# A scheduler's price for a one-pass matmul: 2,400 columns a microsecond, or what the trace shows

## The chip, the cores and the metric

The kernel runs on one core of a Trainium2 chip. The metric is device microseconds (us) of one execution. The trace is one profiled execution on the same core; its times are us from the first instruction. TensorE (PE) multiplies, VectorE (DVE) and ScalarE (ACT) do elementwise work, GpSimd (POOL) does small tensors and issues some DMAs, SyncE (SP) issues the weights' DMAs.

## The reference

Three transformer layers over 256 tokens of width 1024, all in fp32, one after the other:

```
block 1: h = rms_norm(x); u,q,k,v = split(h @ w_in)
         y = [pool_mixer(u), causal attention(q,k,v, 8 heads, T5 bias)] @ w_out
         x = x + rms_norm(y); x = x + rms_norm(conv_ffn(rms_norm(x)))
         x = x + (p @ w_ple) * sigmoid(x @ w_ple_gate)
block 2: u = x @ w_in; y = [short conv, sliding-window attention with sinks] @ w_out
         x = layer_norm(a*x + y); x = layer_norm(a*x + swiglu(x))
block 3: u = x @ w_in; y = [gated linear attention, latent attention with rope] @ w_out
         x = layer_norm(a*x + y); x = layer_norm(a*x + swiglu(x))
```

Nearly all work is fp32 matrix products of 256 tokens with weight matrices, which are read once from HBM (158 MB).

## The kernel before

Each fp32 product is made of three one-pass products in the short format fp32r (`mm3`): both operands are split into a rounded part hi and a rest lo, and hi*hi, hi*lo and lo*hi are added in PSUM. Weights come in units of 512 KB (`get`, l.488): SP's DMA fills one of four buffers `raw`; a cast makes hi (`hl<-raw`, by ACT or, as an alternative, by DVE, where its name is CAST), and a DVE subtraction makes lo (`hl<-raw,hl`). Ten split units (`hl`) form a ring. A chunk of activations against weights (`achunk`) is 24 matmuls of 128x256 (`ps<-hT,hl`); row products and the FFNs also use 128x512 (`ps<-hl,hT`, `ps<-hl,yh`).

In the attention of blocks 1 and 2 a pair of heads follows the chunk pair that makes its q and k. A head (`head`, l.741) is: q·k on PE (`ps<-wk,wk` in block 1, `ps<-g,g` in block 2), a row maximum on DVE (`ISA`), exponential and scaling on ACT and DVE (`g`), three transposes on PE (`ps<-c_ident,g`), evacuation (`pt`), and the product with v (`ps<-pt,vp`). Between q·k and the transposes PE works on chunks of the next weights: I call those matmuls filler. k of a pair is evacuated from PSUM by DVE (`wk<-ps,g`, wk_80; q is wk_82).

All calls are recorded first (`Recorder`). `cost` (l.133) gives each instruction an estimated duration. `add` (l.163) joins matmuls that follow each other on one PSUM tile into a group until the group's estimate reaches `BLOCK` = 0.7 us. `issue` (l.245) is a list scheduler: it sums PE's estimates to due times for all other work, then picks again and again the instruction that can start first by its own clock, on PE within 16 us of the next one in program order; a hi cast goes to DVE where its estimated end there is over 0.2 us earlier (`worth`, l.310). Every engine's instructions are then emitted from l.412 in the order of those estimated starts, so nearly all rows of the trace carry L412. The estimate decides the order only; the waits of the chip are real.

Of the kernel before, what the change touches and what calls it, by code (L numbers as in the profile page):

```python
# [96 lines left out]
class Recorder:  # L97
# [35 lines left out]
    def cost(self, eng, method, out, k, ins):  # L133

        n = out.free_size()
        if method == "dma_start":
            b = out.size() * 4 if callable(out.size) else out.size * 4
            return (1.05 if eng == "POOL" else 0.1), None, b / 360e3
        if eng == "PE":
            if method == "transpose":  # L140
                return n * 2 / 2400.0, None, 0
            m = ins[0].free_size()
            if ins[-1].dtype != F32:
                return max(n, 2 * m) / 2400.0, None, 0
            return (max(4 * n, 4 * m) if n > 32 else 90) / 2400.0, None, 0
        psum = any(x.space == PSUM for x in ins)
        if eng == "ACT":
            d = ((61 if psum else 112) + n) / 1200.0
            for p in ("bias", "scale", "accum_out"):
                if isinstance(k.get(p), bass.AP) and p != "scale":  # L150
                    d += 0.09
            f = k.get("func")
            return d, TABLE.get(f), 0
        if eng == "DVE":
            sc = 0.0625 * sum(isinstance(k.get(p), bass.AP) for p in ("scalar", "scalar1", "scalar2")) * (method != "tensor_tensor_reduce")
            if method in ("tensor_scalar", "tensor_copy", "memset") and not psum and out.space != PSUM:
                return sc + (66 + n / 2) / 960.0, None, 0
            return sc + (66 + n) / 960.0, None, 0
        if method == "memset":
            return 0.04 + n / 1900.0, None, 0  # L160
        return 0.14 + n * 2.15e-3 + (0.4 if k.get("op") == ALU.pow else 0), None, 0
# [1337 lines left out]
```

## Time and profile before

| what | us |
|---|---|
| runs | 878.39, 880.99, 881.13 (median 880.99) |
| the profiled execution | 879.77 |
| its span, first to last instruction | 878.0 |
| PE busy | 861.4 (98%) |
| DVE busy | 672.1 (77%) |
| ACT busy | 505.8 (58%) |
| POOL busy | 62.8 (7%) |

The mean granted TensorE clock is 0.995 of full. Blocks lie at about 0 to 290 us (attention to 100), 290 to 600 (attention 337 to 380) and 600 to the end (its mixers 608 to 656). Matmuls overlap in the trace, so the time of one is read from the start of one row to the start of the next, not from its duration.

### The profile page before, as it was taken

The page shows a single profiled execution, that of the slowest core. Times are in us where ns is not written, and L with a number is a line of the kernel's source. Part 1 is how long each engine was busy: PE and PEld are TensorE (multiplying, and loading weights), DVE is VectorE, ACT ScalarE, POOL GpSimd, SP SyncE. Part 2 cuts the span into 40 slices and gives each one's busy share as a digit, 9 for nine tenths or more (in the row PEclk, how much of TensorE's full clock was granted, in tenths as well). Part 3 has the DMA queues.
Part 4 walks back from the last instruction along what each step waited for, and adds up shares of the span by engine and source line. Part 5 has one row for each costly group of instructions (what it writes and reads, how often), then busy time and mean ns, then how long its engine had stood idle before and what let it go on. Part 6 is the DMA issues. An engine that isn't in the chain of part 4 may idle for free.

```text
span 878.0 us, 14363 instructions
## 1 busy us (share of the span) xinstructions
PE 861.4 (98%) x5182; PEld 740.2 (84%) x5182; DVE 672.1 (77%) x1421; ACT 505.8 (58%) x1086; POOL 62.8 (7%) x99
## 2 busy tenths in 40 slices
PE   8999999999999999999999999999999999999996
PEld 6898788888888889988888888888878888888885
DVE  5898889988884888868877776668996887666644
ACT  5488666665554567745655555446764666555521
POOL 2500100000000000001000000012421100000000
PEclk9999999999999999999999999999999999999998
DMA  8668574776663676527766656536542686666501
GB/s 297 200 190 263 171 245 143 221 224 188 191 213 97 179 222 206 177 66 237 257 201 190 192 185 189 176 107 210 166 137 76 233 270 191 190 189 185 185 19 48
DMA packets 45767, 160.81 MB, mean 183 GB/s; under 512 B 5544, under 2 KB 6360, under 8 KB 45696
## 3 DMA queue, kind: packets, MB, share of 16 engines
q1 hardware_dynamic: 42624, 151.21, 55.0%
q0 software_dynamic: 2640, 8.10, 2.9%
q8 instruction: 40, 0.66, 0.3%
q10 hardware_dynamic: 432, 0.58, 0.2%
q14 instruction: 31, 0.25, 0.1%
HBM read 158.43 MB, written 1.44 MB: 182 GB/s over the span
## 4 chain that ended last, share of the span: by engine, by line
PE 90%; DVE 3%; DMA 3%; issue 2%; ACT 1%; SPq 1%; POOL 0%; POOLq 0%; DVEq 0%
PE ps L412 90%; DMA raw<-in_w_dram 2%; DVE g L412 1%; DVE hl L412 1%; SPq L412 1%; DMA wk<-in_pT_dram 1%; ACT g L412 1%; DVE wk L412 1%; POOL sm L412 0%; DVE x L412 0%; POOLq L1495 0%; ACT L412 0%; ACT wk L412 0%; ACT hl L412 0%; DVE sm L412 0%
## 5 line engine op out<-in xcount | busy, mean ns | idle before, releaser
L412 DVE TENSOR_TENSOR hl<-raw,hl 128x512 fp32r<-128x512 f32 (+1 forms) x570 | 377.3, 689 | 45.0 <-ACT hl L412 39.3
L412 PE MATMUL ps<-hT,hl 128*128 128x512 f32 (+1 forms) x2400 | 401.5, 325 | 2.1 <-ACT hl L412 1.5
L412 PEld LDWEIGHTS ps<-hT,hl 128*128 128x128 f32 x2400 | 350.6, 190 | 44.9 <-issue 2.3
L412 ACT ACTIVATE hl<-raw 128x512 fp32r<-128x512 f32 (+1 forms) x518 | 309.4, 623 | 104.5 <-PE ps L412 65.4
L412 PE MATMUL ps<-hl,yh 128*128 128x512 f32 (+2 forms) x1146 | 259.4, 379 | 1.7 <-DVE yh L412 1.7
L412 PEld LDWEIGHTS ps<-hl,yh 128*128 128x128 f32 x1146 | 202.7, 188 | 40.9 <-DVE yh L412 2.3
L412 PE MATMUL ps<-hl,hT 128*128 128x512 f32 (+2 forms) x720 | 166.0, 385 | 1.1 <-ACT hl L412 1.0
L412 PEld LDWEIGHTS ps<-hl,hT 128*128 128x128 f32 x720 | 129.8, 188 | 27.2 <-ACT hl L412 2.4
L412 ACT ACTIVATE g<-ps 128x256 f32<-128x256 f32 (+6 forms) x156 | 59.4, 388 | 97.0 <-PE ps L412 96.7
L412 DVE TENSOR_TENSOR g<-ps,g 128x256 f32<-128x256 f32 x112 | 47.5, 424 | 49.9 <-ACT g L412 49.7
L412 POOL TENSOR_TENSOR sm<-sm,c_mhalf 128x1 f32<-128x1 f32 (+2 forms) x19 | 18.2, 957 | 515.9 <-DVE sm L412 515.9
L412 ACT ACTIVATE g<-g 128x256 f32<-128x256 f32 (+1 forms) x76 | 31.7, 423 | 16.4 <-DVE g L412 13.0
L412 ACT ACTIVATE yh<-g 128x256 fp32r<-128x256 f32 x57 | 23.6, 416 | 29.2 <-DVE g L412 29.2
L412 DVE CAST hl<-raw 128x512 fp32r<-128x512 f32 (+1 forms) x52 | 23.2, 449 | 17.4 <-PE ps L412 14.7
L412 ACT ACTIVATE wk<-wk,sm 128x1024 f32<-128x1024 f32 (+1 forms) x8 | 9.0, 1127 | 47.3 <-DVE sm L412 47.3
L412 DVE SCALAR_TENSOR_TENSOR wk<-x,ps 128x1024 f32<-128x1024 f32 (+2 forms) x9 | 9.7, 1073 | 32.2 <-PE ps L412 32.2
L412 ACT ACTIVATE g<-g,sm 128x256 f32<-128x256 f32 (+1 forms) x66 | 28.9, 456 | 7.2 <-DVE sm L412 6.9
L412 DVE TENSOR_TENSOR yh<-g,yh 128x256 fp32r<-128x256 f32 x66 | 27.7, 422 | 0.6 <-ACT yh L412 0.5
L412 DVE SCALAR_TENSOR_TENSOR g<-g,c_fm,g 128x255 f32<-128x255 f32 (+2 forms) x52 | 24.7, 480 | 0.9
L412 ACT ACTIVATE hT<-ps 128x512 fp32r<-128x512 f32 x25 | 14.2, 597 | 16.8 <-PE ps L412 16.7
L412 ACT ACTIVATE wk<-ps 128x1024 f32<-128x1024 f32 (+4 forms) x14 | 9.8, 704 | 23.5 <-PE ps L412 21.7
L412 PE MATMUL ps<-c_ident,g 128*128 128x128 f32 (+2 forms) x118 | 19.3, 276 | 1.5 <-DVE g L412 1.4
(121 smaller groups left out, 438.5 us busy)
## 6 DMA issues: line engine op xcount, KB each, us to landing
raw<-in_w_dram SPq DMA_DIRECT2D x277, 512.0 KB, 4.1
row<-in_rows_dram POOLq DMA_DIRECT2D x11, 512.0 KB, 5.3
raw<-in_w_dram SPq DMA_DIRECT2D x4, 432.0 KB, 3.2
x<-in_x_dram SPq DMA_DIRECT2D x2, 512.0 KB, 8.3
row<-vd POOLq DMA_DIRECT2D x8, 128.0 KB, 5.5
raw<-in_w_dram SPq DMA_DIRECT2D x3, 256.0 KB, 3.3
raw<-in_w_dram SPq DMA_DIRECT2D x2, 384.0 KB, 3.3
wk<-in_xT_dram SPq DMA_DIRECT2D x1, 512.0 KB, 7.3
```

The lines of the kernel that those rows point to most:

```text
L412: o.names.append(getattr(e, method)(*map(placed, a), **{p: placed(x) for p, x in k.items()}))
```

## The change

One line of `cost`: the estimate of a one-pass product (moving operand of n columns, stationary operand of m).

```
             m = ins[0].free_size()
             if ins[-1].dtype != F32:
-                return max(n, 2 * m) / 2400.0, None, 0
+                return max(n, 2 * m + 14) * 0.4427e-3, None, 0
             return (max(4 * n, 4 * m) if n > 32 else 90) / 2400.0, None, 0
```

For 128x256 with m = 128 the estimate goes from 0.1067 to 0.1195 us, for 128x512 from 0.2133 to 0.2267 us. A group of `BLOCK` = 0.7 us of 128x256 matmuls closes at 6 (0.717) instead of 7 (0.747), so a chunk of 24 is four groups of 6 instead of 7, 7, 7, 3. Transposes and the two-engine estimates keep their numbers. The instructions are the same but for the hi casts: 77 of them are on DVE now, 52 before. PE's order differs in the attention of blocks 1 and 2, around transposes of rows and at the start of block 3; in the FFNs PE's order is the same and other engines' orders differ.

First place: block 1, PE, the first pair of heads. hl_67 and hl_68 are chunks of the next weights, wk_80 and wk_82 the heads' k and q, g_94 the first head's probabilities.

```order
-L412 MATMUL ps<-hT_77,hl_67 128x256 x14
+L412 MATMUL ps<-hT_77,hl_67 128x256 x12
 L412 MATMUL ps<-wk_80,wk_82 128x128
 L412 MATMUL ps<-wk_80,wk_82 128x256
 L412 MATMUL ps<-wk_80,wk_82 128x128
 L412 MATMUL ps<-wk_80,wk_82 128x256
-L412 MATMUL ps<-hT_77,hl_67 128x256 x10
-L412 MATMUL ps<-hT_77,hl_68 128x256 x21
+L412 MATMUL ps<-hT_77,hl_67 128x256 x12
+L412 MATMUL ps<-hT_77,hl_68 128x256 x18
 L412 MATMUL ps<-c_ident,g_94 128x128 x3
```

q·k stands two matmuls earlier, and 30 matmuls instead of 31 stand between it and the first transposes.

On DVE the same place, before: the evacuation of k (wk_80), then up to the first row maximum (ISA).

```order
L412 TENSOR_TENSOR hl_68<-raw_66,hl_68 128x512
L412 TENSOR_TENSOR wk_80<-ps,g_102 128x256
L412 TENSOR_TENSOR yh_86<-g_107,yh_86 128x256
L412 TENSOR_TENSOR hl_70<-raw_64,hl_70 128x512
L412 SCALAR_TENSOR_TENSOR g_107<-g_106,g_103 128x256
L412 TENSOR_TENSOR hl_69<-raw_63,hl_69 128x256
L412 ISA g_94,sm_116<-ps,row_83 128x128
```

And now:

```order
L412 TENSOR_TENSOR hl_68<-raw_66,hl_68 128x512
L412 TENSOR_TENSOR yh_86<-g_107,yh_86 128x256
L412 TENSOR_TENSOR hl_70<-raw_64,hl_70 128x512
L412 SCALAR_TENSOR_TENSOR g_107<-g_106,g_103 128x256
L412 TENSOR_TENSOR hl_69<-raw_63,hl_69 128x256
L412 SCALAR_TENSOR_TENSOR g_106<-g_105,g_104 128x256
L412 TENSOR_TENSOR wk_80<-ps,g_102 128x256
L412 TENSOR_TENSOR hl_71<-raw_65,hl_71 128x512
L412 TENSOR_TENSOR hl_69<-raw_63,hl_69 128x256
L412 TENSOR_TENSOR yh_87<-g_107,yh_87 128x256
L412 TENSOR_TENSOR hl_70<-raw_64,hl_70 128x512
L412 ISA g_94,sm_116<-ps,row_83 128x256
```

The evacuation of k stands behind five instructions that it stood ahead of, and four more stand between it and the row maximum.

Second place: POOL at the end of block 1's attention. sm_150 to sm_161 are the small power operations of the norms' scales, wk_81 the load of p.

```order
 L412 TENSOR_TENSOR sm_154<-sm_153,c_mhalf 128x1
+L412 DMA wk_81<-in_pT_dram 128x512
 L412 TENSOR_TENSOR sm_157<-sm_156,c_mhalf 128x1
-L412 DMA wk_81<-in_pT_dram 128x512
 L412 TENSOR_TENSOR sm_161<-sm_160,c_mhalf 128x1
```

The load of p is issued ahead of the power operation that it stood behind.

Third place: block 2, PE, the second pair of heads. g_104 and g_102 are the probabilities of its two heads, pt and vp the product with v.

```order
-L412 MATMUL ps<-hT_77,hl_70 128x256 x7
+L412 MATMUL ps<-hT_77,hl_70 128x256 x6
 L412 MATMUL ps<-c_ident,g_104 128x128 x3
-L412 MATMUL ps<-hT_77,hl_70 128x256 x14
+L412 MATMUL ps<-hT_77,hl_70 128x256 x12
 L412 MATMUL ps<-c_ident,g_102 128x128 x3
-L412 MATMUL ps<-hT_77,hl_70 128x256 x3
 L412 MATMUL ps<-pt_179,vp_178 128x256 x3
 L412 MATMUL ps<-pt_179,vp_178 128x128 x3
```

The transposes stand one matmul earlier for the first head and three for the second.

## Rows read from the trace of the kernel before

**Rows 1.** The page: busy time by engine; two of the costliest groups (casts).
```profile
PE 861.4 (98%) x5182; PEld 740.2 (84%) x5182; DVE 672.1 (77%) x1421; ACT 505.8 (58%) x1086; POOL 62.8 (7%) x99
...
L412 ACT ACTIVATE hl<-raw 128x512 fp32r<-128x512 f32 (+1 forms) x518 | 309.4, 623 | 104.5 <-PE ps L412 65.4
...
L412 DVE CAST hl<-raw 128x512 fp32r<-128x512 f32 (+1 forms) x52 | 23.2, 449 | 17.4 <-PE ps L412 14.7
```

**Rows 2.** Waits of PE: what for; us in total, times, longest.
```profile
PE ps L412 <- DVE g L412: 2.8, 3, 1.5
PE ps L412 <- ACT hl L412: 2.4, 3, 1.5
```

**Rows 3.** Windows: us, busy time (instructions) of each engine, clock, DMA share, GB/s.
```profile
340.00:380.00 40.00, 39.99 (x328) 37.55 (x326) 35.55 (x111) 28.89 (x82) 1.79 (x5) 1.00 0.46 148
...
620.00:660.00 40.00, 38.41 (x611) 31.22 (x610) 38.03 (x107) 27.99 (x79) 14.01 (x17) 1.00 0.47 148
700.00:740.00 40.00, 40.00 (x220) 34.42 (x219) 32.65 (x64) 25.70 (x56) 0.00 (x0) 1.00 0.72 236
```

**Rows 4.** Timeline of PE, block 1: start, us, engine, line, operation, count.
```profile
43.30 0.93 PE L412 MATMUL ps<-wk,wk 64*128 64x128 f32 x8
44.16 3.98 PE L412 MATMUL ps<-hT,hl 128*128 128x256 f32 x31
47.97 0.82 PE L412 MATMUL ps<-c_ident,g 128*128 128x128 f32 x6
...
62.03 3.98 PE L412 MATMUL ps<-hT,hl 128*128 128x256 f32 x31
65.85 0.49 PE L412 MATMUL ps<-c_ident,g 128*128 128x128 f32 x3
```

**Rows 5.** Timeline of DVE, block 1, up to the first head's row maximum.
```profile
30.98 0.85 DVE L412 CAST hl<-raw 128x512 fp32r<-128x512 f32 x1
...
38.85 0.42 DVE L412 SCALAR_TENSOR_TENSOR wk<-ps,g 128x256 f32<-128x256 f32 x1 [0.28 <-PE ps L412]
...
41.91 0.41 DVE L412 TENSOR_TENSOR wk<-ps,g 128x256 f32<-128x256 f32 x1
42.24 0.69 DVE L412 TENSOR_TENSOR yh<-g,yh 128x256 fp32r<-128x256 f32 x1
...
44.25 0.29 DVE L412 CUSTOM_DVE_ANT_0 g<-ps,row 128x128 f32<-128x128 f32 x1
```

**Rows 6.** Timeline of ACT, block 1: the scaling of the probabilities before the transposes.
```profile
47.01 1.19 ACT L412 ACTIVATE g<-g,sm 128x256 f32<-128x256 f32 x3
...
65.07 1.19 ACT L412 ACTIVATE g<-g,sm 128x256 f32<-128x256 f32 x3
```

**Rows 7.** Timeline of ACT, block 2: the same scaling.
```profile
343.27 0.79 ACT L412 ACTIVATE g<-g,sm 128x256 f32<-128x256 f32 x2
...
354.93 0.50 ACT L412 ACTIVATE g<-g,sm 128x256 f32<-128x256 f32 x1
```

**Rows 8.** Timeline of PE, block 2: transposes of a pair's other head.
```profile
344.46 0.52 PE L412 MATMUL ps<-c_ident,g 128*128 128x128 f32 x3
...
355.43 0.49 PE L412 MATMUL ps<-c_ident,g 128*128 128x128 f32 x3
```

**Rows 9.** Timeline of POOL ahead of the load of p.
```profile
96.36 0.93 POOL L412 TENSOR_TENSOR sm<-sm,c_mhalf 128x1 f32<-128x1 f32 x1 [6.17 <-DVE sm L412]
```

**Rows 10.** The chain that ended last, in order of time: start, us, what.
```profile
97.25 5.79 DMA wk<-in_pT_dram
```

**Rows 11.** Timeline of PE: where it waits, with the wait in brackets.
```profile
103.42 2.58 PE L412 MATMUL ps<-hl,yh 128*128 128x512 f32 x10 [1.73 <-DVE yh L412]
105.83 1.04 PE L412 MATMUL ps<-c_ident,wk 128*128 128x128 f32 x8
...
625.88 0.61 PE L412 MATMUL ps<-c_ident,g 128*96 128x128 f32 x4 [0.94 <-DVE g L412]
...
629.68 1.05 PE L412 MATMUL ps<-c_ident,g 128*96 128x128 f32 x8 [0.43 <-DVE g L412]
```

More of the change, by code (lines that the diff above doesn't have):

```diff
@@ L143, in cost @@
             if ins[-1].dtype != F32:
-                return max(n, 2 * m) / 2400.0, None, 0
+                return max(n, 2 * m + 14) * 0.4427e-3, None, 0
             return (max(4 * n, 4 * m) if n > 32 else 90) / 2400.0, None, 0
```

## The prediction

> **What bounds the kernel now.** I read the page's busy times first: PE is busy 861.4 us of the span of 878.0, every other engine has room over the whole [rows 1]. Then the waits of PE: 2.8 us for DVE's `g`, 2.4 for ACT's `hl` [rows 2], and one wait of 1.73 us for p at 103.42 [rows 11]; 6.9 us in these together. That is the most that a better order can win, since the matmuls stay the same. Then the windows: in an FFN (700 to 740) PE is busy 40.00 of 40 us and DVE 32.65; in the attention of block 2 39.99 and 35.55; at the start of block 3 PE falls to 38.41 and DVE is at 38.03, so there DVE bounds [rows 3]. Last the timelines of PE, DVE and ACT around each attention head, to see by how much PE's operands are ready before PE takes them. The reader is to see that PE's queue hardly ever waits, and that in the attention it does so by a hair: operands come just in time.
>
> **The change part by part.** Nothing is computed that was not; only order changes, and 25 more hi casts go to DVE. So each term is a wait of PE that appears, or one that goes.
>
> *The estimate itself.* 31 matmuls of 128x256 take from 44.16 to 47.97, 0.123 us each with the handover to the transposes [rows 4]. The old estimate was 0.1067, the new one is 0.1195: the plan's PE now runs nearly as the chip's. The Trainium skill (TensorE: Matmul & The Clock Gate, "Wait — 56ns, not 53.3ns?") gives a start-to-start of columns by 2.4 GHz plus about 2.5 ns for a warm array, 0.109 us for 256 columns as an estimate; by it the old number would be right and the new one 10% too long. The row disagrees, and the measurement decides. By the page's number the plan would now give PE too little filler, and by the row it gives what the plan thinks right; either way less than before.
>
> That is what I expect to cost time. The scheduler fills PE between q·k and the transposes with as many matmuls as it believes the softmax to take. With 0.1067 it put 31 there, which lasted 3.81 us on the chip; with 0.1195 it puts 30 or fewer. The softmax has not become faster, so the old error of PE's price covered an error of the softmax's.
>
> *Block 1, first pair.* q·k starts at 43.30 [rows 4]; k's evacuation, its last operand, ran from 41.91 for 0.41 us [rows 5], ready at 42.32, a margin of 0.98. After: PE comes two matmuls earlier (2 x 0.123), at 43.06. On DVE the evacuation stands behind five more instructions. Four of them took 42.24 to 44.25, 2.01 us, the fifth I count at 0.33, the spacing of 41.91 to 42.24 for its shape: 2.34. Against it, the cast that took 0.85 is replaced by one of the usual 0.45, and DVE's gap of 0.28 can be filled [rows 1, 5]. The evacuation is ready at about 42.32 + 2.34 - 0.40 - 0.28 = 43.98, and PE waits 0.9 (0 if the five do not hold it up, 1.6 if nothing is saved).
> Four more instructions then stand before the row maximum, two subtractions of weights, half a subtraction and one of `yh`, near 1.95 us by the same rows, so it starts at about 45.9 rather than 44.25. The transposes need the first scaling on ACT, which ended about 47.45 (47.01 and a third of 1.19) [rows 6], 3.2 after the row maximum; so 49.1 after. PE, late by the first wait, comes to them after q·k and 30 matmuls: 43.98 + 0.86 + 30 x 0.123 = 48.5. It waits 0.6. First pair: 1.5.
>
> *Block 1, later pairs.* At 65.85 the transposes follow 31 matmuls that began at 62.03 [rows 4]; their operand ended near 65.5 on ACT (65.07 and a third of 1.19) [rows 6], a margin of 0.3. Now 24 matmuls stand there: 7 x 0.123 = 0.86 earlier, a wait of 0.55. Two places have this pattern (here and at the last pair, where 18 matmuls of 512 columns become 12 and one product with v): 1.1. Block 1 together +2.6; bounds 0 (DVE and ACT come earlier by as much) and +4.
>
> *Block 2.* The second head's transposes at 355.43 [rows 8] start in the moment in which ACT ends their operand, 354.93 + 0.50 [rows 7]. In the new order they stand three matmuls earlier, 0.37 of wait; two pairs are like this, 0.7. In the first pair the transposes at 344.46 [rows 8] stand nine matmuls and the product with v earlier, over 1.1 us; their operand ended at 344.06 (343.27 + 0.79) [rows 7], a margin of 0.40: 0.7. Together +1.4; bounds 0 and +2.5.
>
> *The load of p.* POOL issues it at 97.25, behind a power operation that began at 96.36 [rows 9]; it takes 5.79 us [rows 10], and PE waits 1.73 for it [rows 11]. Issued ahead of the power it lands 0.89 earlier. PE's new order also puts four matmuls of 512 columns before the product with p, at (105.83 - 103.42) / 10 = 0.24 each, 0.96 [rows 11]. Both together remove the wait. But the transposes at 105.83 need that power and a chain behind the landing; if they stay there, only the 0.96 is won, if they come 0.89 earlier all of 1.73. The power now stands behind the issue, so I take 0.2 of it: -1.15; bounds -1.73 and 0.
>
> *Start of block 3.* DVE is busy 38.03 of 40 us [rows 3]; between 608 and 652 it gets two or three more casts, at 0.449 [rows 1] +0.9 to +1.35, and subtractions of weights move ahead of the rope's copies that the transposes at 625.88 and 629.68 wait for. I take +1.2. Lower bound: those two waits go, -(0.94 + 0.43) = -1.37 [rows 11]. Upper: a cast beside POOL took 0.85 [rows 5], and POOL is busy 14.01 us of that window [rows 3]; 3 x 0.85 = +2.55. The Trainium skill (GPSIMD Engine Reference, the table of its properties) says that GpSimd's interfaces to SBUF are shared with VectorE; the cast's 0.85 against 0.449 agrees, and by that rule +2.55 would be the likelier end.
>
> *What I cost at nothing.* The other casts that move: in the FFNs DVE has 7 us of room in 40 and PE none [rows 3], and 10 casts there are 4.5 us. If that cover were gone, PE would wait for `hl`. Moved transposes of x rows: DVE's order moves with them; bounds 0 and +1.5.
>
> Sum: +2.6 + 1.4 - 1.15 + 1.2 = +4.05. On the profiled execution's 879.77 us that makes 883.8. That execution lies 1.2 below the median of the runs shown, 880.99, and between their ends.
>
> **The rivals.**
> Faster: the right price lets the plan release producers in time. Its place is where PE is waited for now: the wait for p goes wholly (1.73), and the two at block 3 with it (1.37): 879.77 - 3.1 = 876.7. For it speaks that the load is in fact issued earlier; against it that DVE in block 3 gets more work, not less. It decides if the attention's operands come earlier by more than PE does (0.4 to 0.9 us a pair), so that no new wait opens.
> No change: PE's 861.4 us stay, new waits of a few tenths are filled where the ends of products overlap, and the gain at p (1.15) pays for the rest: 879 to 881. For it speaks that PE waits under 7 us now, although hundreds of instructions stand in an order that was planned with a wrong price; against it the margins of 0 to 0.4 us.
> Much slower: DVE becomes the bound through the attention of block 1 and block 3 as well, since casts and subtractions stand before the row maxima: the upper ends, 4 + 2.5 + 0 + 2.55 = 9, 888.8. Against it: DVE still has 4.5 us of room in 40 in block 2's attention [rows 3], and a queue that is late there catches up.
>
> **How the numbers follow.** About 0.3% (2.6 us) is what a measurement of this kernel can tell from no change. Forecast, a loss of 2.6 to 6 us: 0.40. No change: 0.35, since half of the terms rest on margins that I read to 0.1 us and DVE's queue may catch up. Faster: 0.17, its working gives -3.1, beyond that bound. Much slower: 0.08. So faster 0.17, same 0.35, slower 0.48. The range reaches to 877.5, into the faster rival, and to 888.5, near the sum of the upper ends; the forecast's own range is 882.4 to 886.
>
> **What would show it right or wrong.** Right: PE's waits for DVE and ACT in 40 to 80 and 340 to 370 rise to some 4 us, the first at q·k near 43; the wait before the product with p is gone, and the transposes after it wait a little; DVE in 620 to 660 is at 39 or more. Wrong: the transposes of the attention still start without a wait, because the scaling on ACT ends earlier than it does now, or the time falls under 877.5, which would need waits gone that I hold to be DVE's own work.

## The result and the profile after

| | before | after |
|---|---|---|
| median of the runs on one chip (us) | 880.65 (4 runs, 878.39 to 881.13) | 892.08 (4 runs, 890.02 to 894.56) |
| ratio | | 1.0137, 95% interval 1.0114 to 1.0160 |
| span of the profiled execution | 878.0 | 892.7 |
| mean granted clock in it | 0.995 | 0.990 |
| waits of PE, sum of the view | 7.7 | 15.4 |

The kernel became 11.4 us slower: the direction forecast, near three times the 4.05 forecast, and outside the range of 877.5 to 888.5. The profiled execution of after is the slowest of its four, 894.56, and lies 14.7 above that of before in its span.

From the page of after, busy time by engine and the group of casts on DVE, against [rows 1]:

```profile
PE 868.9 (97%) x5182; PEld 744.9 (83%) x5182; DVE 679.6 (76%) x1439; ACT 497.2 (56%) x1068; POOL 62.3 (7%) x99
...
L412 DVE CAST hl<-raw 128x512 fp32r<-128x512 f32 (+1 forms) x77 | 33.1, 434 | 23.2 <-PE ps L412 20.8
```

The same 5182 matmuls keep PE busy 7.5 us longer: some of them ran at a lower clock. By the mean granted clocks, 0.990 of 892.7 us and 0.995 of 878.0, an estimate of 4.5 us at most goes there. The rest is waiting. Most of the loss is not the clock: the run of after at 890.02 us had a mean granted clock of 0.996 and was still 9.4 slower than the median of before. The longest of PE's waits in after, against [rows 2] (what for; total, times, longest):

```profile
PE ps L412 <- ACT g L412: 4.5, 5, 3.4
PE ps L412 <- DVE wk L412: 4.3, 2, 3.9
...
```

Two waits stand out, 3.9 for `wk` and 3.4 for ACT's `g`. The first is at q·k of block 1's first pair. Timeline of PE in after, against [rows 4]:

```profile
45.84 1.66 PE L412 MATMUL ps<-wk,wk 64*128 64x128 f32 x8 [3.93 <-DVE wk L412]
47.42 5.68 PE L412 MATMUL ps<-hT,hl 128*128 128x256 f32 x30
52.94 0.49 PE L412 MATMUL ps<-c_ident,g 128*128 128x128 f32 x3
```

Two things are to be seen: the wait, and that q·k and 30 matmuls then take 7.10 us up to the transposes. Before they took 47.97 - 43.30 less one matmul of 0.123, 4.55 [rows 4]; so 2.55 us go in the clock. Windows of after show it (us, busy time of PE, PEld, DVE, ACT, POOL, then the granted clock), and with them those of [rows 3]:

```profile
45.00:51.00 6.00, 5.16 (x24) 4.51 (x25) 5.21 (x21) 3.47 (x12) 1.04 (x2) 0.50 0.96 266
340.00:380.00 40.00, 39.32 (x328) 37.16 (x327) 34.86 (x103) 26.56 (x72) 1.94 (x5) 1.00 0.51 157
620.00:640.00 20.00, 16.46 (x118) 15.27 (x118) 19.13 (x44) 16.81 (x35) 7.72 (x10) 0.97 0.69 217
640.00:660.00 20.00, 19.92 (x472) 15.62 (x473) 17.63 (x39) 6.05 (x14) 7.14 (x11) 0.86 0.39 120
```

After PE's idle stretch the granted clock is 0.50, the level of 1.2 GHz, for the six microseconds shown; after the idle stretch in 620 to 640 it falls to a mean of 0.86 in the next 20. What PE waited for is on DVE. Its timeline in after, against [rows 5]:

```profile
29.95 0.43 DVE L412 CAST hl<-raw 128x512 fp32r<-128x512 f32 x1 [1.13 <-DMA raw<-in_w_dram]
...
43.43 0.41 DVE L412 TENSOR_TENSOR yh<-g,yh 128x256 fp32r<-128x256 f32 x1
43.76 0.68 DVE L412 TENSOR_TENSOR hl<-raw,hl 128x512 fp32r<-128x512 f32 x1
44.36 0.41 DVE L412 SCALAR_TENSOR_TENSOR g<-g,g 128x256 f32<-128x256 f32 x1
44.70 0.41 DVE L412 TENSOR_TENSOR hl<-raw,hl 128x256 fp32r<-128x256 f32 x1
45.03 0.41 DVE L412 SCALAR_TENSOR_TENSOR g<-g,g 128x256 f32<-128x256 f32 x1
45.37 0.41 DVE L412 TENSOR_TENSOR wk<-ps,g 128x256 f32<-128x256 f32 x1
...
47.58 0.41 DVE L412 CUSTOM_DVE_ANT_0 g<-ps,row 128x256 f32<-128x256 f32 x1
...
48.47 0.16 DVE L412 TENSOR_SCALAR sm<-sm 128x2 f32<-128x2 f32 x1
```

k's evacuation starts at 45.37, before at 41.91: 3.46 later. The five instructions ahead of it take 1.94 (43.43 to 45.37). Most of the rest comes from the start of the stretch, where DVE now waits 1.13 for the transfer of a weight that it is to cast; what follows that cast was 1.75 late. On ACT the exponentials stand behind two casts that wait for a transfer as well:

```profile
47.98 1.15 ACT L412 ACTIVATE hl<-raw 128x512 fp32r<-128x512 f32 x2 [2.08 <-DMA raw<-in_w_dram]
49.04 0.49 ACT L412 ACTIVATE g<-g,sm 128x256 f32<-128x256 f32 x1
...
49.53 0.39 ACT L412 ACTIVATE g<-g,sm 128x128 f32<-128x128 f32 x1
```

These casts cost little here: the operand that the first exponential needs from DVE (`sm`, at 48.47) is ready at 48.63, and it starts at 49.04. The delay is DVE's, whose first row maximum starts at 47.58, before at 44.25 [rows 5].

Block 3 has a wait of the same kind. PE in after, against [rows 11]:

```profile
632.65 4.03 PE L412 MATMUL ps<-hl,yh 128*128 128x384 f32 x21
640.08 1.91 PE L412 MATMUL ps<-c_ident,g 128*96 128x128 f32 x8 [3.40 <-ACT g L412]
```

DVE in after, then in before:

```profile
634.28 1.89 DVE L412 TENSOR_TENSOR hl<-raw,hl 128x512 fp32r<-128x512 f32 x3
636.09 0.75 DVE L412 TENSOR_TENSOR g<-g,g 128x256 f32<-128x256 f32 x2
...
637.37 0.21 DVE L412 COPY g<-g 128x128 f32<-128x128 f32 x1
```

```profile
621.16 2.30 DVE L412 TENSOR_TENSOR hl<-raw,hl 128x512 fp32r<-128x512 f32 x3
...
624.66 0.75 DVE L412 COPY g<-g 128x128 f32<-128x128 f32 x1
```

From the chain that ended last in after, the way from DVE's `g` to the transposes:

```profile
636.60 0.43 ACT g L412
...
637.16 1.02 POOL g L412
...
639.39 0.59 ACT g L412
```

Three subtractions of weights (`hl<-raw,hl`) stand ahead of the `g` that ACT, POOL and again ACT work on before the transposes at 640.08. They stood at this place before as well. New are three more ahead of them: from PE's matmuls of 16x256 (620.70; before 609.99) to the first copy of the rope (`g<-g`) DVE does 12 subtractions, before 9, and the copy comes 16.7 us after those matmuls, before 14.7. The other 1.5 us of the delay lie behind the copy: the transposes start 2.7 after it, before 1.2, since they stand in another order and wait for ACT first.

Worked out from PE's two timelines, by the time at which it reaches the same matmul, after is 6.9 us behind at 100, 7.5 at 330, 9.0 at 370, 10.1 at 430, 10.8 at 610, 15.2 at 630 and 14.7 at the end.

### The profile page after: what moved, and what is told of

Same layout as the page of the kernel before. It is cut to its first block, busy times and chain, and to the rows that moved or that the text cites. A ratio compares the mean times of both kernels' runs of the same rounds, so it can differ in the third digit from the quotient of the medians.

```text
span 892.7 us, 14411 instructions
## 1 busy us (share of the span) xinstructions
PE 868.9 (97%) x5182; PEld 744.9 (83%) x5182; DVE 679.6 (76%) x1439; ACT 497.2 (56%) x1068; POOL 62.3 (7%) x99
## 4 chain that ended last, share of the span: by engine, by line
PE 81%; DMA 6%; DVE 5%; ACT 3%; issue 3%; SPq 1%; POOL 1%; POOLq 0%; DVEq 0%; ACTq 0%
PE ps L412 81%; DMA raw<-in_w_dram 5%; DVE hl L412 2%; DVE g L412 1%; ACT g L412 1%; SPq L412 1%; ACT hl L412 1%; DMA wk<-in_pT_dram 1%; DVE wk L412 1%; DVE yh L412 1%; POOL g L412 1%; ACT wk L412 0%; ACT yh L412 0%; ACT L412 0%; DVE x L412 0%
## 5 line engine op out<-in xcount | busy, mean ns | idle before, releaser
L412 DVE TENSOR_TENSOR hl<-raw,hl 128x512 fp32r<-128x512 f32 (+2 forms) x570 | 380.0, 693 | 39.8 <-ACT hl L412 33.2
L412 ACT ACTIVATE hl<-raw 128x512 fp32r<-128x512 f32 (+1 forms) x493 | 296.6, 625 | 119.1 <-PE ps L412 69.8
L412 ACT ACTIVATE g<-ps 128x256 f32<-128x256 f32 (+5 forms) x155 | 59.3, 388 | 100.2 <-PE ps L412 99.4
L412 DVE CAST hl<-raw 128x512 fp32r<-128x512 f32 (+1 forms) x77 | 33.1, 434 | 23.2 <-PE ps L412 20.8
L412 ACT ACTIVATE yh<-g 128x256 fp32r<-128x256 f32 x62 | 26.0, 419 | 34.8 <-DVE g L412 34.7
L412 PE MATMUL ps<-c_ident,g 128*128 128x128 f32 (+2 forms) x118 | 21.3, 298 | 5.8 <-ACT g L412 4.5
L412 ACT ACTIVATE hT<-ps 128x512 fp32r<-128x512 f32 x26 | 14.7, 599 | 17.5 <-PE ps L412 17.5
```

What stands on the lines that cost most here:

```text
L412: o.names.append(getattr(e, method)(*map(placed, a), **{p: placed(x) for p, x in k.items()}))
```

## The experiments

Ratios are to the kernel before on the same chip, with the 95% interval; 4 to 11 runs each. Diffs are against the changed kernel.

**One instruction at a time.** First theory: the order of single instructions on DVE, k's evacuation behind the five (e1) and the cast that waited for its transfer (e2), or both (e3). Beside it the 25 casts (e4).

```
e1  in the finished order, k's evacuation (210) moved ahead of the five:
+        late = {157, 310, 172, 295, 188}
+        order[p0:p + 1] = [o for o in order[p0:p + 1] if o.i not in late] + [o for o in order[p0:p] if o.i in late]
     (cut: whatever depends on one of `late` joins it)
e2  +    if (i, c) in ((7, 0), (7, h)): nc.ops[-1].alts = {}      (its cast on ACT, as before)
e3  e1 and e2
e4  +    if 2 * i + c // h in ON_DVE: o.eng = "DVE" ...; o.alts = {}   (each cast on the engine of before)
```

> The changed kernel (892.1) with one VectorE instruction moved: in block 1's first head pair k's evacuation stands ahead of the five instructions that the change put before it, as in the kernel before; all else as changed. Theory A (VectorE's queue order is what costs: non-urgent work stands before the evacuation that PE waits for): the five took 1.94 us (43.43 to 45.37), so PE's wait at the first q-k falls from 3.93 to about 2.0, the stretch at the 1.2 GHz level after it (6.8 us in the profile) goes or shrinks, and the time is 2 to 5 us less: 887 to 890. Rival B (VectorE is late by itself, whatever stands there, and the time is made up later): 892, within 1.

> The changed kernel with one hi cast of the start (half of the eighth weight unit) back on ScalarE. In the changed kernel VectorE stood 1.13 us at that cast, waiting for its DMA, with the evacuations of block 1 queued behind. Theory A: VectorE reaches k's evacuation 1.1 to 1.75 us earlier, PE's first long wait falls to 2.2 to 2.8, the time to about 889 to 891. Rival B (the next thing in VectorE's queue waits for the same DMA, so the gap only moves): 892, and a gap of about 1 us before another instruction near 30 us.

> The changed kernel with both edits, the evacuation first and the cast on ScalarE. Theory A: the two delays add up to 3.7 us, so the wait of 3.93 at the first q-k nearly goes (under 0.8), no stretch at the 1.2 GHz level follows it, and the time is 885 to 887.5: what is left over the kernel before is block 2 (1.4) and block 3 (4.5). Rival B: 890 or more, since the waits that go come back at the transposes behind.

> The changed kernel with every one of the 570 hi casts on the engine that the kernel before gave it (52 on VectorE); the matmul price, the groups and the scheduler are as changed and plan the rest around it. Theory A (order of the queues by the plan's clock, casts only a small part): 889 to 891, the first q-k still waits over 2 us since the five instructions stay ahead of the evacuation. Rival C (the 25 casts that went to VectorE are the cost, in the start and in block 3): 882 to 884.

Measured: e1 1.0123 [1.0108, 1.0138], e2 1.0135 [1.0113, 1.0157], e3 1.0141 [1.0117, 1.0165], e4 1.0107 [1.0082, 1.0132]. The theory fell. In e1 the wait at q·k is short, as meant, and a new one comes at the transposes; PE, then DVE and ACT, in e1 (the edits shift the line number):

```profile
41.61 0.93 PE L419 MATMUL ps<-wk,wk 64*128 64x128 f32 x8 [1.06 <-DVE wk L419]
...
48.55 0.84 PE L419 MATMUL ps<-c_ident,g 128*128 128x128 f32 x3 [2.24 <-ACT g L419]
```

```profile
45.29 0.42 DVE L419 CUSTOM_DVE_ANT_0 g<-ps,row 128x256 f32<-128x256 f32 x1
...
46.18 0.16 DVE L419 TENSOR_SCALAR sm<-sm 128x2 f32<-128x2 f32 x1
```

```profile
46.75 0.49 ACT L419 ACTIVATE g<-g,sm 128x256 f32<-128x256 f32 x1
```

The five instructions now stand, with four that the change put there, between k's evacuation (41.14) and the first row maximum (45.29): 4.15 us, before 2.34 [rows 5], in after 2.21. So the wait moved on along DVE's own queue. The two casts on ACT add 0.4: `sm` is ready at 46.34, the exponential starts at 46.75. In e2 q·k still waits 3.50, in e4 3.04. e4's ratio lies 0.3% below the changed kernel's with overlapping intervals: the casts are at most a small part. In the profiles of e1 and e3 the mean granted clock is 0.995, as in before, and they lose as much as after: the loss does not need a lower clock than before had.

**Which block.** The new price only while block 1, or block 3, is recorded.

```
+                if self.new:
+                    return max(n, 2 * m + 14) * 0.4427e-3, None, 0
+                return max(n, 2 * m) / 2400.0, None, 0
```

> The new price only for matmuls recorded in block 1, the old one in blocks 2 and 3. Theory A (the loss is made where the order of the attention and mixers changes): block 1's part, 3 to 4 us of waits at the first head pair and at the load of p, and up to 3.4 us more where the waits are followed by a stretch at the 1.2 GHz level: 884.5 to 888 beside 880.5 to 881.5 for the kernel before; from 300 us on PE runs as in the kernel before, shifted by a constant. The prediction's sizes (2.6 less 1.15) would give 882 to 883.

> The new price only for matmuls recorded in block 3. Theory A: the 4 to 5 us by which PE falls back between 605 and 640 in the changed kernel come here alone: 884.5 to 887, with a wait of 2 to 4 us before the transposes that follow the key products. The prediction's size for block 3 (+1.2) would give 882 to 883; Rival D (block 3 is late in the changed kernel only because the blocks ahead of it have changed): within 1 of the kernel before.

Measured: block 1 885.27, 1.0067 [1.0042, 1.0093]; block 3 883.76, 1.0046 [1.0023, 1.0069]; before 880.04. So 5.2 us lie in block 1 (with the load of p) and 3.7 in block 3, and 2.5 of the 11.4 are left for block 2 and what the blocks do to each other. q·k in e5 waits 3.37, the transposes in e6 3.38.

**The prediction's own reason.** It held that PE gets too little filler, since groups close at six matmuls. e7 has the new price with the old groups, e8 the old price with the new ones.

```
e7, e8: a group's size has an estimate of its own, apart from the duration
+            gd = max(n, 2 * m) / 2400.0                   (e7)
+            gd = max(n, 2 * m + 14) * 0.4427e-3           (e8, with the old price for the duration)
-        if eng == "PE" and self.open is not None and self.open.dur < self.block and \
+        if eng == "PE" and self.open is not None and self.open.grp < self.block and \
```

> The scheduler's clock runs by the new price, but matmuls are joined into groups by the old one (7, 7, 7, 3 of a chunk). Theory A (the clock of the plan reorders VectorE, ScalarE and their casts): most of the loss stays, 888 to 892. Rival F, the prediction's own reason (groups of 6 cut the filler between q-k and transposes from 31 to 30 matmuls and less): the loss goes, 881 to 884, as the filler is 31 again.

> The old price for the scheduler's clock, but groups as in the changed kernel (6, 6, 6, 6). Theory A: little is lost, what the shorter filler costs in block 2 (1.4) and at a pair of block 1: 881.5 to 884. Rival F: most of the loss is here, 888 to 892.

Measured: e7 890.87, 1.0129 [1.0094, 1.0164], with 31 matmuls of filler again and a wait of 3.71 at q·k; e8 879.50, 1.0003 [0.9983, 1.0023], with 30 of filler, a wait of 0.62 there and none at the transposes. The reason is refuted: filler and groups cost nothing within 0.2%, and the price in the scheduler's clock nearly all.

**More instructions by hand.** e9 puts nine DVE instructions in block 1 and the splits in block 3 back behind the chain that PE waits for; e13 does it on ACT's queue too. e11 lets no split of a weight (cast or subtraction) on DVE start earlier than 7 us before its due time; e12 is that with the old price.

```
e9   +MOVES = [({157, 310, 172, 295, 188}, 210), ({320}, 229), ({188, 293, 174, 312}, 232), ({3159, 3161, 3166, 3168}, 2906), ({3172, 3174}, 2923)]
e13  +MOVES = [({157, 310}, 210), ({295, 320}, 229), ({359, 361}, 230), ({293, 174, 312}, 232), ({3159, 3161, 3166, 3168, 3172, 3174}, 2928)]
     (cut: each set, with what depends on it and what follows that on another engine, goes behind the instruction named)
e11, e12
+                        if o.unit and n == "DVE":
+                            return max(r, o.due - LEAD)
     (cut: `unit` marks the casts and subtractions of weights, LEAD is 7.0)
```

> The changed kernel with VectorE's order of the kernel before put back at two places, every other engine's order as changed. In block 1's first pair nine instructions that the change put ahead of the first row maximum (splits of later weights, yh, g) stand behind where they stood before; in block 3 the splits of three weight units stand behind the rope's copies. Theory A2 (what costs is work that nobody waits for, put on VectorE ahead of the chain that PE waits for, where VectorE has no room): the waits at the first q-k and at its transposes, 3.9 us together in the changed kernel and 3.3 in the run with only k's evacuation moved, fall to under 1.5; the 3.4 at block 3's transposes to under 1.8; no stretch at 1.2 GHz follows: 884 to 887. Rival G (VectorE has more to do in these stretches altogether, so the wait only moves on, as it did when five were moved): 890 to 892.

> The changed kernel with the work that nobody waits for yet put behind the chain at the two worst places, on VectorE and on ScalarE: in block 1's first pair seven splits and subtractions on VectorE behind k's evacuation, the row maxima or the reciprocals, and ScalarE's two casts of the unit that waits for its DMA behind the exponentials; in block 3 six splits behind the rope and the evacuations. Nothing is moved that ScalarE's queue waits for. Theory A2: the first q-k waits at most 2.8 (it was 3.93), its transposes under 1, block 3's first transposes under 1 and the next under 1; the stretches at 1.2 GHz after them go: 884 to 888. Rival G (these engines have too much to do there in any order): 890 to 893.

> The changed kernel with one rule added to the scheduler: VectorE may not start a split of weights (cast or subtraction) more than 7 us before its due time by the plan. Theory A2: the splits no longer stand ahead of block 3's rope chain and of the softmax in block 2, so block 3's loss goes (4 us) and block 2's (1.4); in block 1's first pair the plan still has most of the nine ahead: 884 to 888. It could cost where the weights then come late for PE (waits of PE for VectorE's hl): 890 or more.

> The kernel before with the same rule, splits of weights on VectorE at most 7 us before due. If the greedy splits also cost the kernel before its 1.4 us of waits at block 3, it gains up to 1.5 us: 878.5 to 880; if the splits come late for PE it loses, 881 to 884.

Measured: e9 893.17, 1.0161 [1.0134, 1.0187]; e13 901.15, 1.0249 [1.0222, 1.0276]; e11 896.82, 1.0200 [1.0170, 1.0230]; e12 881.20, 1.0015 [0.9997, 1.0033]. e9, e13 and e11 failed as repairs; e12 equals the kernel before within its interval. In e9 the first transposes wait 3.30 for ACT, whose queue stands at a cast of `yh` for a `g` that I had moved back on DVE; ACT in e9:

```profile
45.87 0.42 ACT L424 ACTIVATE yh<-g 128x256 fp32r<-128x256 f32 x1 [2.65 <-DVE g L424]
...
47.23 0.49 ACT L424 ACTIVATE g<-g,sm 128x256 f32<-128x256 f32 x1
```

In e13 the first transposes wait only 0.84, and the second head's 6.00, because on ACT their scaling (`g`) stands behind a cast whose transfer lands late; ACT, PE and DVE in e13, and the transfer, from the chain that ended last:

```profile
47.45 1.14 ACT L424 ACTIVATE hl<-raw 128x512 fp32r<-128x512 f32 x2
53.37 0.63 ACT L424 ACTIVATE hl<-raw 128x512 fp32r<-128x512 f32 x1 [4.78 <-DMA raw<-in_w_dram]
...
54.27 0.39 ACT L424 ACTIVATE g<-g,sm 128x128 f32<-128x128 f32 x1
```

```profile
54.72 0.90 PE L424 MATMUL ps<-c_ident,g 128*128 128x128 f32 x3 [6.00 <-ACT g L424]
```

```profile
48.10 1.29 DVE L424 TENSOR_TENSOR hl<-raw,hl 128x512 fp32r<-128x512 f32 x2 [1.45 <-ACT hl L424]
```

```profile
49.85 3.43 DMA raw<-in_w_dram
```

The transfer itself is not slow, 3.43 us; it is issued late. The two casts that I had put behind the exponentials start at 47.45; DVE's subtractions behind them wait 1.45 for them, and in the chain the transfer follows those subtractions. The splits share four buffers `raw` with the transfers, so a split that I put late held up the weights behind it.

The order is one piece over three queues and the transfers. Moving part of it moves the wait.

**The ratio of prices.** Next theory: the old price was wrong for PE alone and right against the others, since the other engines are slower on the chip than the plan believes too; with a dearer PE the plan thinks DVE and ACT have time, and puts splits of weights that nobody needs yet ahead of evacuations and softmax. The new price is kept, and estimates of other engines are raised by 1.12, as 0.1195 to 0.1067.

That the other engines are slower than their estimates was not tested, and the rows of after speak against it for the commonest instructions. `cost` gives a subtraction of 128x512 on DVE (66 + 512) / 960 = 0.602 us, and the one at 43.76 is followed by the next at 44.36; a cast of 128x512 on ACT 0.520, and two take from 47.98 to 49.04, 0.53 each; an exponential of 256 columns 0.487, and from 49.04 to the next are 0.49. What the runs below can show is the ratio, not its cause.

```
+        if eng in ("DVE", "ACT", "POOL", "SP"):           (e10)
+        if eng in ("DVE", "POOL"):                        (e14)
+        if eng in ("ACT",):                               (e15)
+        if eng in ("SP",):                                (e16)
+        if eng in ("DVE", "ACT", "POOL"):                 (e18)
+            dur, xfer = dur * 1.12, xfer * 1.12
     (cut: where DVE's rise, so does the price of a cast that may go to DVE)
e17:
-                return max(n, 2 * m + 14) * 0.4427e-3, None, 0
+                return max(n, 2 * m + 14) / 2400.0, None, 0
```

> The new matmul price, and every estimate of VectorE, ScalarE, GpSimd and of the transfers raised by the same 12% (0.1195 over 0.1067), the fixed latencies and windows as they are. Theory A2 with its cause (before, PE was planned too fast by as much as the others run late on the chip; the plan is good when the ratio of the engines is right, not PE's time): most of the loss goes, 879 to 884. Rival H (a right PE time is bad by itself, through the fixed constants): 888 to 892.

> The new matmul price, and VectorE's and GpSimd's estimates raised by the same 12%; ScalarE and transfers as they are. If VectorE's ratio to PE is what matters (it is the engine whose queue held the evacuations): 880 to 885. If another engine's: 888 to 892.

> The new matmul price, and ScalarE's estimates raised by 12%; it sends casts from ScalarE to VectorE (911 instead of 991 of ScalarE's instructions stay). If VectorE is the engine short of time, this is worse than the changed kernel: 892 to 897. If ScalarE's ratio matters: 882 to 887.

> The new matmul price, and the transfers' estimates raised by 12%, the engines' as they are. If the splits that wait for a DMA ahead of evacuations and exponentials are the main cost: 883 to 887. If VectorE's ratio is: 888 to 892.

> Half of the change alone: columns (or the floor of twice the weights' columns + 14) at the old 2.4 per ns, so products of 256 columns are raised from 0.1067 to 0.1125 and those of 512 stay at 0.2133. Ratio theory (what costs is PE's price against the others', whatever part raises it, in proportion): products of 256 columns stand in the attention's q, k, v; a part of the loss, 2 to 6 us over the kernel before, 882 to 886. Rival (the price has a threshold, past which one unlucky order comes; below it nothing is lost): 879 to 881. Rival (the floor alone makes the loss, since the attention holds the 256-column products): 890 to 893.

> The new price of PE, and the estimates of VectorE, GpSimd and ScalarE raised by 1.12, those of the weights' transfers left as they are. Theory (the three compute engines' prices against PE's decide; transfers do not): the whole loss goes, 879 to 882, as with all four raised. Rival (the 4 us that VectorE's and GpSimd's prices alone left belong to the transfers, which the plan then believes to land in time for splits that it puts ahead): it stays at 884 to 886.

| kernel | estimates raised beside PE's | median | ratio |
|---|---|---|---|
| after | none | 892.08 | 1.0137 [1.0114, 1.0160] |
| e16 | transfers | 889.17 | 1.0125 [1.0095, 1.0154] |
| e15 | ACT | 889.96 | 1.0126 [1.0104, 1.0148] |
| e14 | DVE, POOL | 884.95 | 1.0062 [1.0037, 1.0086] |
| e18 | DVE, POOL, ACT | 879.24 | 0.9989 [0.9974, 1.0004] |
| e10 | all four | 880.83 | 1.0008 [0.9990, 1.0026] |
| e17 | none; PE's raised for 256 columns alone, by 5% | 884.94 | 1.0051 [1.0031, 1.0071] |

The whole loss goes when DVE's, POOL's and ACT's estimates rise with PE's; the transfers' estimate is not needed. DVE and POOL alone win back over half; ACT alone 1 to 2 us, with overlapping intervals, but beside them the rest. e17, with 0.1125 in place of 0.1195, loses under half; it is no clean measure of the size of the raise, since in its profile the product with p alone waits 3.58, before 1.73 [rows 11], and the ten matmuls there take 3.95 instead of 2.41. e18 isn't the old order again: it has 95 casts on DVE and 24 matmuls of filler. In it (PE, then ACT):

```profile
41.52 0.93 PE L414 MATMUL ps<-wk,wk 64*128 64x128 f32 x8 [0.77 <-DVE wk L414]
42.38 3.14 PE L414 MATMUL ps<-hT,hl 128*128 128x256 f32 x24
45.85 0.66 PE L414 MATMUL ps<-c_ident,g 128*128 128x128 f32 x3 [0.33 <-DVE g L414]
```

```profile
39.57 0.61 ACT L414 ACTIVATE hl<-raw 128x512 fp32r<-128x512 f32 x1
42.88 0.42 ACT L414 ACTIVATE yh<-g 128x256 fp32r<-128x256 f32 x1 [2.69 <-DVE g L414]
43.97 0.40 ACT L414 ACTIVATE g<-g,sm 128x128 f32<-128x128 f32 x1 [0.68 <-DVE sm L414]
```

No cast of a weight stands on ACT between 40.2 and the exponentials, where after and e1 have two that wait for a transfer. On DVE the weights' subtractions that stand ahead can be counted in each timeline:

| kernel | ahead of k's evacuation | ahead of the first row maximum | wait at q·k | ratio |
|---|---|---|---|---|
| before | 24 | 26 | none | 1 |
| e8 | 24 | 26 | 0.62 | 1.0003 |
| e18 | 24 | 26 | 0.77 | 0.9989 |
| e10 | 24 | 25 | 1.21 | 1.0008 |
| e14 | 25 | 26 | 2.62 | 1.0062 |
| e17 | 25 | 27 | 2.15 | 1.0051 |
| e5 | 26 | 29 | 3.37 | 1.0067 |
| e7 | 26 | 28 | 3.71 | 1.0129 |
| after | 26 | 29 | 3.93 | 1.0137 |

More splits ahead, a longer wait at q·k. It fits most of the runs left out too: e4 26 and 28 with 3.04, e15 25 and 28 with 3.59, e16 25 and 28 with 2.63. In block 3 the same count, from PE's matmuls of 16x256 to the rope's first copy, is 9 in before and e8 (first wait of the transposes behind 0.94 and 1.54), 10 in e18 and e10 (1.52 and 2.29), 11 in e17 (2.32), 12 in e14, e6 and after (3.38, 3.38 and 3.40). It is not the count alone: e9, with 24 and 26 by hand, loses 1.6%, for ACT's queue was left as planned; e13, with 24 and 25, loses 2.5%; e11, with 24 and 28, waits 2.49.

## Why the prediction was wrong

The direction was right; the size, the range and the reason were not.

**The reason.** The step "The scheduler fills PE between q·k and the transposes with as many matmuls as it believes the softmax to take ... with 0.1195 it puts 30 or fewer" failed. e8 has 30 and loses nothing, e18 has 24 and loses nothing, e7 has 31 and loses all. I looked for the price's effect on PE's queue. It is on the queues of DVE and ACT: a plan in which PE takes longer leaves them time, and they fill it with splits that are early, ahead of what PE is about to ask for. That the old price covered another error is not shown: raising the prices of DVE, POOL and ACT with it undoes the loss (e18), but the rows give no sign that the commonest of those prices are too low.

**Block 1, +2.6 forecast, +1.45 with the load of p.** e5, which holds both, gives 5.2. The term mis-sized is the wait at q·k, 0.9 forecast and 3.93 in the profile. The five instructions were sized about right (2.34 forecast, 1.94). Wrong were the credits of 0.40 and 0.28: DVE isn't earlier but later there, by 1.75 after its wait for a transfer. e2 shows that this cast alone isn't it, since with the cast back on ACT q·k still waits 3.50. And the sum had no term for the clock, 2.55 us in the profile. The transposes' waits that I added (0.6 and 1.1) did not come: PE, late itself, found the operands ready.

**Block 2, +1.4 forecast.** The profile shows 1.4 from 330 to 370 and PE idle 0.68 us in 340 to 380. The size fits by luck, since the places are others: the transposes that I forecast to wait, the second heads', do not. The first heads' do, by 0.19, 0.29 and 0.20 in three pairs; two of them:

```profile
345.51 3.85 PE L412 MATMUL ps<-hT,hl 128*128 128x256 f32 x30
349.56 0.55 PE L412 MATMUL ps<-c_ident,g 128*128 128x128 f32 x3 [0.19 <-ACT g L412]
...
357.61 3.85 PE L412 MATMUL ps<-hT,hl 128*128 128x256 f32 x30
361.76 0.52 PE L412 MATMUL ps<-c_ident,g 128*128 128x128 f32 x3 [0.29 <-ACT g L412]
```

From the start of the 30 matmuls to the transposes are 4.05 and 4.15 us, and 4.05 in the third pair; at 0.123 each they take 3.69. That is 1.18 of the 1.4. I cost the FFNs at nothing; the start of block 2's gives another 1.1 at 430, where PE waits 1.15 for a `g` on DVE.

**The load of p, -1.15 forecast.** Next to nothing came. PE in after, against [rows 11], then the transfer, from the chain that ended last:

```profile
110.29 2.64 PE L412 MATMUL ps<-hl,yh 128*128 128x512 f32 x10 [0.82 <-DVE yh L412]
113.28 1.32 PE L412 MATMUL ps<-c_ident,wk 128*128 128x128 f32 x8 [0.35 <-DVE wk L412]
```

```profile
103.80 6.12 DMA wk<-in_pT_dram
```

The wait went from 1.73 to 0.82. But the transposes behind it, which did not wait, now do, so that the ten matmuls take 2.99 up to them instead of 2.41, and by the same matmul PE is 6.9 us behind ahead of this place and 6.8 after it. The transfer is issued 6.55 later than before (97.25), 0.3 earlier than PE's lag; it takes 6.12 instead of 5.79 [rows 10], and that is gone. At 134.23 PE waits another 0.54, for a `wk` on ACT; that wait is new.

**Block 3, +1.2 forecast.** e6 gives 3.7. I charged the casts' own time on a busy DVE. DVE was in fact less busy there, 36.76 us in 620 to 660 where I had named 39 or more as a sign of being right. The loss was a chain: three more subtractions ahead of the rope, a changed order of the transposes, a wait of 3.40, and the low clock behind it.

**The rivals.** "Much slower" named the right engine and, at 888.8, came nearest, with a chance of 0.08. Its mechanism, splits ahead of what PE waits for, is what the trace shows, but DVE didn't become the bound of the stretch throughout: in the profile the loss sits mostly in two waits with the clock behind them.

Shown: the ratio of the price of PE to those of DVE, POOL and ACT makes the loss (e10, e18), in block 1 and block 3 (e5, e6), not groups or filler (e7, e8). Argued from timelines only: that early splits on both queues are the way in which it does; my repairs by hand (e1, e3, e9, e13, e11) should have confirmed it and did not, so which pieces of the order cost how much stays open. Open too is why the raised prices help, as the rows show the commonest of them right already, and how far the time scatters from one order to the next: every variant is one order, and apart from e17 no neighbouring price was run. No version was faster than the kernel before beyond its interval; e18 and e8 equal it.

## What to carry to other kernels

In this list scheduler the prices worked as ratios. Putting PE's price right made the plan worse, and raising the other engines' by the same factor undid it, although their commonest prices agreed with the trace. So a price that agrees with the trace does not by that give a better order: try a new price for one engine also with the others scaled alike. And a wait that is priced at its own length is priced too low where PE's clock falls behind it: look at the granted clock after every stall of a few microseconds. Last, a split that is put late holds its buffer and so the next transfer (e13).

## What the hardware showed that I had not expected

- After PE stood still for 3.93 us the granted clock was 0.50 for the next six microseconds, and the matmuls behind took 2.55 us more. In e5 a wait of 3.37 was followed by 0.50 in 45 to 47; in e1 waits of 1.06 and 2.24, seven microseconds apart, left it at 1.00 in every window from 38 to 58. The length of the wait at q·k alone does not decide: in e14 one of 2.62 was followed by 0.57 in 43 to 47, in e16 one of 2.63 by 1.00 from 42 to 58.
- A transfer that is issued late costs more than it takes: in e13 it took 3.43 us, a cast on ACT waited 4.78 us for it, and PE's transposes behind that cast 6.00.
